# A hybrid decoder layer whose order a planner sets: other planning numbers, other pairs of outputs in PSUM banks, and two lists of tiles turned

## The chip, the cores and the metric

The kernel runs on one core of one Trainium2 chip. Its metric is the device time of one execution in microseconds, the median of several. A core has five engines that run their own instruction streams: TensorE (PE; its weight loads are shown as PEld), VectorE (DVE), ScalarE (ACT), GpSimd (POOL) and SyncE (SP), which here only issues DMAs. They meet in semaphores. Matmul results go to PSUM, eight banks of 512 fp32 numbers in each partition; everything else lies in SBUF.

## The reference

One decoder layer on 512 tokens of width 2048, in fp32. The conditioning vector `c` makes six modulation vectors through `w_ada`, 2048 x 12288 numbers, the largest matrix of the first stage.

```
mod_all = einsum('bd,ldm->lbm', silu(c), w_ada) + b_ada
h = rms_norm(x, norm1_g) * (1 + sc1) + sh1
u = h @ w_in                  # conv group, queries, keys and values of three branches, gates
y_conv = short_conv_mixer(u_b, u_c, u_h, conv_w, conv_b)
k_cmp = compress(rope(kc), cmp_pe_k, cmp_w1_k, cmp_w2_k)      # and v_cmp
y_attn = nsa_attention(q, k_cmp, v_cmp, k_slc, v_slc, k_win, v_win, gates)
x = x + g1 * ([rms_norm(y_conv) | rms_norm(y_attn)] @ w_out)
h = rms_norm(x, norm2_g) * (1 + sc2) + sh2
x = x + g2 * (square(relu(h @ w_ff1)) @ w_ff2)
return rms_norm(x, normf_g)
```

## The kernel before, in words

Every fp32 product is made of three matmuls in fp32r (`mm3`): high part times high part, high times low, low times high. So each weight tile of 128 x 1024 that a DMA brings is first split: ScalarE copies it to the high part, VectorE subtracts that from it for the low part (`weights`, `hilo`).

There are three stages, and each has a recorder of its own, an object of class `Order`, which stands in for the engines: a call is noted down with what it reads and writes, and all of it is put out at `emit`. In between, `plan` runs a list scheduler. It prices each instruction (`price`), gives each a due time (`late`), and always takes the instruction that can begin first. DMAs share one modelled wire, which moves `rate` bytes in a microsecond. The order in which the plan begins them is the order in which they stand on every engine; engines and queues then run in that order, whatever their real times are. Nearly all instructions are recorded, so they bear the line of the recorder's call, L123.

The first stage projects the normed tokens `h` with `w_kv`, `w_cv`, `w_conv`, `w_v` and `w_q` (tiles `raw`, split into `wh`; the compression weights are split into tiles called `sw`, in spare slots). Beside it run the 192 tiles of `w_ada`: SyncE loads one into a ring of tiles `wa`, and VectorE takes its product with `silu(c)` summed along the row (`dot`, a SCALAR_TENSOR_TENSOR `t,late<-wa,cs`, or `t,acc` for the first ones). From `part_done` on that ring has four tiles. A `wa` load carries a slack, `SLACK`: the plan begins it no sooner than so many microseconds after it is ready, its tile being free among other things. `more_ada` puts these loads in, along with the projections, at the places that the plan then moves.

The second stage is attention (scores `s` in three banks, values `pv`, transposes `pt`), with the output product of the convolution half (`pw`, two banks) filled in between. VectorE's first instructions there clear the tile `pc` of the first query block and read the first scores (`p<-s`).

The third stage starts with the output product of the attention half. Its first eight outputs (`pm`) take all eight banks `pf`, one each, for all 512 tokens. The second eight are made by `late_out`, for 256 tokens at a time: the first call for the low half, the second for the high half. An output of 256 tokens takes half a bank, 24 matmuls. The weights are kept in SBUF in between, in tiles called `hl`, `sg`, `gt` and `kw`. `residual` reads the result on VectorE and adds it to `x1`. Then come the two products of the feed-forward part, which are three fifths of the time. Their weight tiles pass through six staging tiles `rw`, taken in turn, as are the banks.

Of the kernel before, what the change touches and what calls it, by code (L numbers as in the profile page):

```python
# [16 lines left out]
P = 128  # L17
# [19 lines left out]
NSIDE = 7  # L37
NWA = 8
NBANK = 6
SLACK = 4.0  # L40
SOON = 10.0
BEHIND = 11.0

# [6 lines left out]
class Order:  # L50
# [2 lines left out]

    class Node:
        __slots__ = ("i", "eng", "call", "cost", "lag", "size", "preds", "succs", "late", "loose", "born",
                     "begin", "ready", "left", "lane", "slack", "due")

    def __init__(self, tc, tag, count, passes=1, pace=0.000456, rate=340e3):  # L60
        self.tc, self.tag, self.count, self.passes = tc, tag, count, passes
        self.lane, self.kept, self.slack, self.wide, self.pace = 0, set(), 0.0, (0.11, 0.00182), pace
        self.rate = rate
        self.nodes, self.past, self.seen, self.rings = [], {}, {}, {}
        self.outer, self.loose, self.due = set(), False, 0.0
        for e in ("tensor", "vector", "scalar", "sync", "gpsimd"):
            setattr(self, e, Order.Engine(self, e, getattr(tc.nc, e)))
# [132 lines left out]
    def plan(self, ideal, t, fixed):  # L200
        nodes = self.nodes
        ends = {}
        for name, by in self.seen.items():
            for i in set(by):
                ends.setdefault(i, []).append(name)
        users = {name: len(set(v)) for name, v in self.seen.items()}
        mine = sorted((n for x in nodes for n in x.born), key=lambda n: int(n.rsplit("_", 1)[1]))
        rank = {n: k for k, n in enumerate(mine)}

        for x in reversed(nodes):  # L210
            move = x.cost + x.lag if not x.size else 2.5 + x.size / self.rate
            x.late = min([nodes[s].late - (move if nodes[s].eng != "tensor" or x.eng != "tensor" else x.cost)
                          for s in x.succs] + [ideal.get(x.i, t + 10.0 - x.due)])

        free = dict.fromkeys(("tensor", "vector", "scalar", "sync", "gpsimd"), 0.0)
        wire = 0.0
        ready = {e: [] for e in free}
        lanes = {}
        for i in fixed or [x.i for x in nodes if x.eng == "tensor" and not x.loose]:
            lanes.setdefault(0 if fixed else nodes[i].lane, []).append(i)  # L220
        for lane in lanes.values():
            lane.reverse()
        slots = sorted([0.0] * (self.count - len(self.outer)))
        given = []
        while slots and len(given) < len(mine):
            given.append(slots.pop(0))
        for x in nodes:
            x.left, x.ready = len(x.preds), 0.0
            if not x.left and (x.eng != "tensor" or x.loose):
                ready[x.eng].append(x)  # L230
        out = []
        while len(out) < len(nodes):
            best = None
            for e in free:
                c = [(x, 0, None) for x in ready[e]]
                if e == "tensor":
                    c = [(x, -1, None) for x in ready[e]]
                    c += [(nodes[q[-1]], k, q) for k, q in lanes.items() if q and not nodes[q[-1]].left]
                for x, k, q in c:
                    at = max(free[e], x.ready + x.slack, wire - 2.0 if x.size else 0.0)  # L240
                    if x.born:
                        last = max(rank[n] for n in x.born)
                        if last >= len(given):
                            continue
                        at = max(at, given[last])
                    key = (at, k, x.late, x.i)
                    if best is None or key < best[0]:
                        best = key, x, q
            (at, *_), x, q = best
            e = x.eng  # L250
            if q is not None:
                q.pop()
            else:
                ready[e].remove(x)
            x.begin = at
            free[e] = at + x.cost
            end = at + x.cost + x.lag
            if x.size:
                wire = max(wire, at + 1.5) + x.size / self.rate
                end = wire + 0.7  # L260
            for n in ends.get(x.i, ()):
                users[n] -= 1
                if not users[n] and (n in rank or n in self.outer) and n not in self.kept:
                    if len(given) < len(mine):
                        given.append(max([end] + given[-1:]))
            for s in x.succs:
                y = nodes[s]
                y.left -= 1
                y.ready = max(y.ready, free[e] if e == y.eng == "tensor" else end)
                if not y.left and (y.eng != "tensor" or y.loose):  # L270
                    ready[y.eng].append(y)
            out.append(x)
        return max(free.values()), out
# [3 lines left out]
def hybrid_layer(ctx: ExitStack, tc: tile.TileContext, a, out):  # L277
# [38 lines left out]
        tc.keep_in_program_order(filler(nc.tensor))  # L316

    xs = [pair(name="x2") for _ in range(NK // 2)]
    nc = order = Order(tc, xs[0].tensor.tag, NMAIN, passes=6, pace=0.000444, rate=410e3)
    order.wide = (0.24, 0.0021)  # L320
    ts = [small.tile([P, T], F32, name="t", tag="t", bufs=5) for _ in range(5)]
    scr, temps = ts[0].bitcast(BF16), cycle(ts[1:])
# [797 lines left out]
    ffp = ffn.enter_context(tc.tile_pool(name="ffp", bufs=2, reuse_waits="tile"))  # L1120
    psf = ffn.enter_context(tc.tile_pool(name="psf", bufs=8, space=PSUM, reuse_waits="tile"))
    HT = T // 2
    rw = cycle([ffp.tile([P, 1024], F32, name="rw", bufs=6) for _ in range(6)])
    hl = cycle([ffp.tile([P, 2048 + 4 * SHIFT], F32R, name="hl", bufs=3) for _ in range(3)])

    class Low:
# [16 lines left out]
    gt = cycle([ffp.tile([P, 2, 2, HT], F32R, name="gt", bufs=3) for _ in range(3)])  # L1143
    gb = cycle([ffp.tile([P, 2, HT], F32R, name="gb", bufs=1)])
    p1s = cycle([ffp.tile([P, HT], F32, name="p1", bufs=3) for _ in range(3)])
    banks = cycle([psf.tile([P, T], F32, name="pf") for _ in range(8)])
    LO, HI = slice(0, HT), slice(HT, T)
    halves = (LO, HI)
    whole = slice(0, T)
# [1 line left out]
    def bankf():  # L1151
        return next(banks)
# [30 lines left out]
    def residual(ps, m, c):  # L1183
        xm = x1[m // 2][:, m % 2, c]
        nc.vector.scalar_tensor_tensor(out=xm, in0=ps, scalar=col(M_G1, m), in1=xm,
                                       op0=OP.mult, op1=OP.add)
        square_into(sacc, xm, c, m == 0)
# [27 lines left out]
            dst = [slot(F32R, name="kw")[:, :1024] for _ in range(2)]  # L1215
        kept.append(hilo(dst, raw_blob(a["w_oa2"][i])))
    def late_out(hf):
        ps = []
        for i in range(8):
            if i % 2 == 0:  # L1220
                ps.append(bankf())
            wh, wl = kept[i]
            for k in range(8):
                s = slice(k * P, (k + 1) * P)
                mm3(ps[-1][:, halves[i % 2]], wh[:, s], wl[:, s], mixa[k][:, 0, halves[hf]],
                    mixa[k][:, 1, halves[hf]], k == 0, k == 7)
        for i in range(8):
            c = halves[hf]
            residual(ps[i // 2][:, halves[i % 2]], 8 + i, c)
            if i % 2:  # L1230
                j = 4 + i // 2
                nc.gpsimd.dma_start(out=x1d[j][:, :, c], in_=x1[j][:, :, c])
# [416 lines left out]
```

## Time and profile before

| | |
|---|---|
| median of 3 executions | 2099.62 us (2099.16 to 2104.02) |
| profiled execution | 2096.75 us |
| its span, first to last instruction | 2095.0 us |
| mean granted TensorE clock | 0.991 |
| ScalarE, GpSimd busy | 1007.7 us (48%), 128.1 us (6%) |
| first stage | to about 557 us |
| attention with half the output product | to about 748 us |
| rest of the output product | to about 845 us |
| feed-forward part | to the end |

The span is what the profile shows of one execution; the execution's own time is 1.75 us longer. Rows of the timeline give start and length in microseconds, engine, line, operation, output and inputs by the program's names, shape, and in brackets how long the engine idled before and what ended that. Rows of waits give the waiting engine, its tile and line, what it waited for, and the total, the number and the longest. "Granted clock" is the share of TensorE's full clock that it was given.

### The profile page before, as it was taken

What the parts mean: (1) busy time and instruction counts of PE and PEld (TensorE: products, weight loads), DVE (VectorE), ACT (ScalarE), POOL (GpSimd) and SP (SyncE); (2) the same over time, 40 slices, a digit from 0 to 9 for tenths busy, and PEclk for the clock granted to TensorE, in tenths of its full rate; (3) what the DMA queues carried; (4) which work ended last, traced back from release to release, by engine and by line L of the source; (5) the groups of instructions that cost most, each with busy time, mean ns of one, the idle gap of its engine ahead of it and who ended that gap; (6) DMA issues with size and microseconds to landing.
All of it is one profiled execution on the core that took longest, in us unless ns stands there. A gap on an engine that the chain in (4) does not pass through costs nothing.

```text
span 2095.0 us, 38213 instructions
## 1 busy us (share of the span) xinstructions
PE 2054.9 (98%) x15038; PEld 1920.0 (92%) x15038; DVE 1885.9 (90%) x3104; ACT 1007.7 (48%) x1465; POOL 128.1 (6%) x244
## 2 busy tenths in 40 slices
PE   9999999999999999999999999999999999999997
PEld 7888787898788779999999999999999999999997
DVE  7999997887898657999999999999999999999998
ACT  4432333232465435776666666666443333333355
POOL 0000000000000001022211121222000000000000
PEclk8999999999999999999999999999999999999999
DMA  8986488888511134476766666668975466476452
GB/s 343 348 325 231 174 294 324 311 292 307 200 63 69 62 134 152 136 227 207 211 210 205 208 214 198 213 206 285 347 274 211 163 248 227 138 254 239 144 181 99
DMA packets 144276, 454.19 MB, mean 217 GB/s; under 512 B 15840, under 2 KB 20320, under 8 KB 144096
## 3 DMA queue, kind: packets, MB, share of 16 engines
q1 hardware_dynamic: 108960, 386.72, 52.7%
q0 software_dynamic: 34048, 63.98, 10.1%
q8 instruction: 118, 1.93, 0.4%
q10 hardware_dynamic: 1088, 1.05, 0.1%
q14 instruction: 62, 0.51, 0.1%
HBM read 383.53 MB, written 68.16 MB: 216 GB/s over the span
## 4 chain that ended last, share of the span: by engine, by line
PE 90%; DVE 4%; DMA 3%; ACT 1%; issue 1%; SPq 0%; DVEq 0%; ACTq 0%
PE pf L123 63%; PE ps L123 19%; PE pw L123 4%; PE pv L123 2%; PE s L123 2%; DMA wa<-in_w_ada 1%; PE pt L123 1%; DMA raw<-in_cmp_w 1%; DVE wh L123 1%; DVE t L123 1%; DMA raw<-in_w_conv 0%; DMA x<-in_xt 0%; DVE x L123 0%; ACT wh L123 0%; DVE vz L123 0%
## 5 line engine op out<-in xcount | busy, mean ns | idle before, releaser
L123 PE MATMUL pf<-tk,hl 128*128 128x256 f32 x10704 | 1218.7, 276 | 0.5 <-ACT t L123 0.5
L123 PEld LDWEIGHTS pf<-tk,hl 128*128 128x128 f32 x10704 | 1217.1, 188 | 0.8 <-ACT t L123 0.7
L123 ACT ACTIVATE hl<-rw 128x1024 fp32r<-128x1024 f32 x269 | 285.7, 1063 | 338.3 <-PE pf L123 291.0
L123 DVE TENSOR_TENSOR hl<-rw,hl 128x1024 fp32r<-128x1024 f32 (+2 forms) x351 | 336.4, 968 | 32.4 <-ACT hl L123 31.9
L123 ACT ACTIVATE hl<-sg 128x1024 fp32r<-128x1024 f32 x180 | 191.1, 1062 | 217.3 <-PE pf L123 170.0
L123 DVE SCALAR_TENSOR_TENSOR t<-wa,cs 128x1024 bf16<-128x1024 f32 x190 | 231.7, 1220 | 30.7 <-DMA wa<-in_w_ada 29.0
L123 PE MATMUL ps<-h_m,wh 128*128 128x512 f32 x1080 | 252.3, 390 | 0.9 <-DVE h_m L123 0.9
L123 PEld LDWEIGHTS ps<-h_m,wh 128*128 128x128 f32 x1080 | 201.1, 188 | 42.4 <-DVE h_m L123 1.3
L123 ACT ACTIVATE wh<-raw 128x1024 fp32r<-128x1024 f32 (+1 forms) x106 | 112.7, 1064 | 257.3 <-PE ps L123 214.8
L123 DVE TENSOR_TENSOR hl<-sg,hl 128x1024 fp32r<-128x1024 f32 (+2 forms) x193 | 188.2, 986 | 27.1 <-ACT hl L123 26.9
L123 PE MATMUL ps<-h,wh 128*128 128x512 f32 x840 | 198.9, 395 | 2.9 <-ACT h L123 2.9
L123 PEld LDWEIGHTS ps<-h,wh 128*128 128x128 f32 x840 | 159.5, 191 | 36.7 <-ACT h L123 3.5
L123 DVE TENSOR_TENSOR wh<-raw,wh 128x1024 fp32r<-128x1024 f32 (+1 forms) x106 | 129.7, 1224 | 21.8 <-ACT wh L123 21.1
L123 DVE TENSOR_TENSOR sg<-sg,rw 128x1024 f32<-128x1024 f32 x120 | 145.8, 1215 | 0.0
L123 DVE SCALAR_TENSOR_TENSOR x<-pf,mod,x 128x256 f32<-128x256 f32 (+1 forms) x280 | 130.0, 483 | 13.5 <-PE pf L123 11.6
L123 POOL DMA_DIRECT2D g<-gt x192 | 101.1, 532 | 424.3 <-ACT hl L123 185.7
L123 PE MATMUL pw<-mix,wh 128*128 128x512 f32 x384 | 110.7, 407 | 0.0
L123 ACT ACTIVATE t<-t 128x512 f32<-128x512 f32 (+3 forms) x131 | 74.8, 571 | 15.9 <-DVE t L123 13.8
L123 DVE TENSOR_TENSOR sg<-rw 128x1024 f32<-128x1024 f32 x60 | 73.1, 1219 | 7.9 <-DMA rw<-in_w_f 4.8
L123 PEld LDWEIGHTS pw<-mix,wh 128*128 128x128 f32 x384 | 69.2, 190 | 10.8 <-issue 0.5
L123 DVE TENSOR_TENSOR rw<-rw 128x1024 f32<-128x1024 f32 x60 | 72.9, 1215 | 0.0
L123 ACT ACTIVATE gt<-t 128x512 fp32r<-128x512 f32 x96 | 60.3, 629 | 18.1 <-DVE t L123 15.2
(217 smaller groups left out, 1775.6 us busy)
## 6 DMA issues: line engine op xcount, KB each, us to landing
rw<-in_w_f SPq DMA_DIRECT2D x263, 512.0 KB, 4.2
wa<-in_w_ada SPq DMA_DIRECT2D x192, 512.0 KB, 6.0
tk<-g SPq DMA_DIRECT2D x114, 512.0 KB, 6.6
g<-gt POOLq DMA_DIRECT2D x192, 256.0 KB, 5.3
raw<-in_w_conv SPq DMA_DIRECT2D x32, 512.0 KB, 4.0
x<-in_xt SPq DMA_DIRECT2D x16, 512.0 KB, 5.7
raw<-in_w_kv SPq DMA_DIRECT2D x16, 512.0 KB, 5.5
raw<-in_w_cv SPq DMA_DIRECT2D x16, 512.0 KB, 5.1
```

The costliest lines, as they stand in the source:

```text
L123: x.i, x.eng, x.call = len(self.nodes), eng, (lambda: real(*args, **kw))
```

## The change

Five edits. `SLACK` goes from 4 to 1. The planner's wire gets two rates in place of one for each stage: 340 thousand bytes a microsecond, and 410 while the modelled wire time is below `rush`; the first stage, which had 410 throughout, now has it for its first 40 modelled microseconds, and its due times always use 340. The other stages had 340 and keep it. In `late_out`, outputs i and i+4 share a bank, where 2j and 2j+1 did. The list of banks begins at its third name, and the list of `rw` tiles runs backwards behind its first.

```
-SLACK = 4.0
+SLACK = 1.0
...
+    RATE, RUSH = 340e3, 410e3
...
-    def __init__(self, tc, tag, count, passes=1, pace=0.000456, rate=340e3):
+    def __init__(self, tc, tag, count, passes=1, pace=0.000456, rush=0.0):
...
-        self.rate = rate
+        self.rush = rush
...
-            move = x.cost + x.lag if not x.size else 2.5 + x.size / self.rate
+            move = x.cost + x.lag if not x.size else 2.5 + x.size / Order.RATE
...
-                wire = max(wire, at + 1.5) + x.size / self.rate
+                wire = max(wire, at + 1.5)
+                wire += x.size / (Order.RUSH if wire < self.rush else Order.RATE)
...
-    nc = order = Order(tc, xs[0].tensor.tag, NMAIN, passes=6, pace=0.000444, rate=410e3)
+    nc = order = Order(tc, xs[0].tensor.tag, NMAIN, passes=6, pace=0.000444, rush=40.0)
...
-    rw = cycle([ffp.tile([P, 1024], F32, name="rw", bufs=6) for _ in range(6)])
+    rw = [ffp.tile([P, 1024], F32, name="rw", bufs=6) for _ in range(6)]
+    rw = cycle(rw[:1] + rw[:0:-1])
...
-    banks = cycle([psf.tile([P, T], F32, name="pf") for _ in range(8)])
+    banks = [psf.tile([P, T], F32, name="pf") for _ in range(8)]
+    banks = cycle(banks[2:] + banks[:2])
...
     def late_out(hf):
-        ps = []
+        ps = [bankf() for _ in range(4)]
         for i in range(8):
-            if i % 2 == 0:
-                ps.append(bankf())
             wh, wl = kept[i]
             for k in range(8):
                 s = slice(k * P, (k + 1) * P)
-                mm3(ps[-1][:, halves[i % 2]], wh[:, s], wl[:, s], mixa[k][:, 0, halves[hf]],
+                mm3(ps[i % 4][:, halves[i // 4]], wh[:, s], wl[:, s], mixa[k][:, 0, halves[hf]],
                     mixa[k][:, 1, halves[hf]], k == 0, k == 7)
         for i in range(8):
             c = halves[hf]
-            residual(ps[i // 2][:, halves[i % 2]], 8 + i, c)
+            residual(ps[i % 4][:, halves[i // 4]], 8 + i, c)
```

The planning numbers move instructions all through the first stage from about its tenth weight tile on; the second stage stands as it was, and the third differs only around `late_out`. Three places follow, each before and then after.

VectorE at the end of the first stage; its last row here is the first of attention. `mix` are the splits of the convolution half, `t,late<-wa,cs` are dots, `wh<-raw` is the low part of a weight tile:

```order
L123 TENSOR_TENSOR mix<-y,mix 128x512 x5
L123 TENSOR_TENSOR wh<-raw,wh 128x1024
L123 TENSOR_TENSOR mix<-y,mix 128x512 x3
L123 SCALAR_TENSOR_TENSOR t,late<-wa,cs 128x1024 x2
L123 TENSOR_TENSOR wh<-raw,wh 128x1024
L123 SCALAR_TENSOR_TENSOR t,late<-wa,cs 128x1024 x5
L123 TENSOR_TENSOR mod<-late 128x16
L123 TENSOR_TENSOR mod<-mod,vec 128x16
L123 MEMSET pc 128x96 x2
```

```order
L125 TENSOR_TENSOR mix<-y,mix 128x512 x6
L125 TENSOR_TENSOR wh<-raw,wh 128x1024
L125 SCALAR_TENSOR_TENSOR t,late<-wa,cs 128x1024 x3
L125 TENSOR_TENSOR wh<-raw,wh 128x1024
L125 SCALAR_TENSOR_TENSOR t,late<-wa,cs 128x1024
L125 TENSOR_TENSOR mod<-late 128x16
L125 TENSOR_TENSOR mod<-mod,vec 128x16
L125 TENSOR_TENSOR wh<-raw,wh 128x1024
L125 MEMSET pc 128x96 x2
```

The last two `wh<-raw` in each are those for the last `w_q` tile and the first tile of the convolution half's output weights, `w_oc`. Seven dots stood between the former and attention, and one stands there now; the three `mix` splits have moved ahead of it.

SyncE at the same place, the last loads ahead of the second stage's first load of `x`:

```order
L123 DMA wa<-in_w_ada 128x1024 x2
L123 DMA raw<-in_w_q 128x1024
L123 DMA wa<-in_w_ada 128x1024 x2
L123 DMA raw<-in_w_q 128x1024
L123 DMA wa<-in_w_ada 128x1024 x2
L123 DMA raw<-in_w_oc 128x1024
L123 DMA wa<-in_w_ada 128x1024 x4
L123 DMA raw<-in_w_oc 128x1024 x2
```

```order
L125 DMA wa<-in_w_ada 128x1024 x2
L125 DMA raw<-in_w_q 128x1024
L125 DMA wa<-in_w_ada 128x1024 x3
L125 DMA raw<-in_w_q 128x1024
L125 DMA wa<-in_w_ada 128x1024
L125 DMA raw<-in_w_q 128x1024 x2
L125 DMA raw<-in_w_oc 128x1024 x3
```

Six `wa` loads stood behind the last `w_q` load, four of them behind the first `w_oc` load; now none does, and between weight loads two or three stand where two did.

TensorE in the first call of `late_out`, from its third output (brackets name the engine whose semaphore a matmul waits for). The weights of the outputs are `hl`, then `sg`, `gt`, and `kw` for three:

```order
L123 MATMUL pf<-mixa,hl 128x256 x21
L123 MATMUL pf<-mixa,sg 128x256 x8
L123 MATMUL pf<-mixa,sg 128x256 [waits DVE_49]
L123 MATMUL pf<-mixa,sg 128x256 x15
L123 MATMUL pf<-mixa,gt 128x256 x24
L123 MATMUL pf<-mixa,kw 128x256 x2
L123 MATMUL pf<-mixa,kw 128x256 [waits DVE_49]
L123 MATMUL pf<-mixa,kw 128x256 x45
```

```order
L125 MATMUL pf<-mixa,hl 128x256 x21
L125 MATMUL pf<-mixa,sg 128x256 x24
L125 MATMUL pf<-mixa,gt 128x256 [waits DVE_49]
L125 MATMUL pf<-mixa,gt 128x256 x23
L125 MATMUL pf<-mixa,kw 128x256 [waits DVE_49]
L125 MATMUL pf<-mixa,kw 128x256 x23
L125 MATMUL pf<-mixa,kw 128x256 [waits DVE_49]
L125 MATMUL pf<-mixa,kw 128x256 x23
```

The waits for VectorE stood inside an output, behind its eighth or second matmul, for the read of the output just before it. Now they stand at an output's first matmul, for the read of the output four earlier.

## The prediction

> **What bounds the kernel now.** I read the page's first lines, then the windows of 50 us, then TensorE's own waits.
>
> ```profile
> span 2095.0 us, 38213 instructions
> ...
> PE 2054.9 (98%) x15038; PEld 1920.0 (92%) x15038; DVE 1885.9 (90%) x3104; ACT 1007.7 (48%) x1465; POOL 128.1 (6%) x244
> ...
> 200.00:250.00 50.00, 48.35 (x230) 39.74 (x229) 48.40 (x67) 20.89 (x25) 0.00 (x0) 1.00 0.39 135
> 250.00:300.00 50.00, 47.59 (x239) 39.19 (x238) 43.02 (x61) 18.86 (x23) 0.00 (x0) 1.00 0.83 303
> 300.00:350.00 50.00, 48.80 (x237) 39.86 (x236) 40.43 (x61) 16.11 (x17) 0.00 (x0) 1.00 0.86 311
> 350.00:400.00 50.00, 48.04 (x237) 39.45 (x236) 41.27 (x63) 14.27 (x19) 0.00 (x0) 1.00 0.86 318
> 400.00:450.00 50.00, 47.95 (x315) 43.77 (x314) 43.01 (x67) 15.06 (x22) 0.00 (x0) 1.00 0.82 290
> 450.00:500.00 50.00, 50.00 (x295) 44.78 (x294) 39.22 (x70) 11.18 (x17) 0.00 (x0) 1.00 0.89 315
> 500.00:550.00 50.00, 50.00 (x223) 41.40 (x222) 44.04 (x64) 18.09 (x25) 0.00 (x0) 1.00 0.73 253
> 550.00:600.00 50.00, 44.83 (x226) 38.24 (x225) 43.28 (x146) 24.91 (x71) 0.00 (x0) 0.90 0.33 116
> ...
> 850.00:900.00 50.00, 49.53 (x432) 49.28 (x431) 46.02 (x96) 37.19 (x69) 1.10 (x2) 1.00 0.39 127
> ```
>
> In the windows, the columns are the stretch, its length, the busy time of TensorE, of its weight loads, VectorE, ScalarE and GpSimd, the granted clock, the DMA share and GB/s. TensorE is busy for 2054.9 of 2095.0 us, so 40.1 us is all that a better order can win, and whatever delays TensorE is paid in full. Behind 850 us its windows are full to within half a microsecond; what is won ahead of that point should be kept. The idle time that this change can touch lies in two stretches: 200 to 450 us has 1.65 + 2.41 + 1.20 + 1.96 + 2.05 = 9.3 us, and 550 to 600 us has 5.2 us, in one piece, with the clock down to 0.90. TensorE's waits name the culprits (columns: total, times, longest):
>
> ```profile
> PE ps L123 <- ACT sw L123: 6.3, 7, 1.6
> PE s L123 <- DVE pc L123: 5.2, 1, 5.2
> PE pf L123 <- DVE x L123: 3.6, 5, 1.3
> ```
>
> The first are the compression weights `sw` in the first stage, the second is the door from the first stage to attention, the third mostly the second half of the output product.
>
> **The change part by part.**
>
> *Names that turn.* The reversed `rw` list and the rotated `banks` list change which name comes first. In the two built programs the tiles stand at the same places in the order of use: the first bank used is bank 0, then 7, 6, 5 and so on in both, and all 277 loads into `rw` go to the same addresses in the same order. So no wait moves and both cost 0. That the first matmul of the output product waits for the same VectorE update in both programs fits.
>
> *The door to attention.* The timeline there:
>
> ```profile
> 537.70 19.20 PE L123 MATMUL ps<-h,wh 128*128 128x512 f32 x84
> 547.90 1.22 DVE L123 TENSOR_TENSOR wh<-raw,wh 128x1024 fp32r<-128x1024 f32 x1
> 551.27 1.06 ACT L123 ACTIVATE wh<-raw 128x1024 fp32r<-128x1024 f32 x1 [3.81 <-PE ps L123]
> 554.90 2.64 ACT L123 ACTIVATE qr<-ps 128x512 f32<-128x512 f32 x4 [2.57 <-PE ps L123]
> 556.74 1.13 PE L123 MATMUL s<-kslc,q 128*128 128x160 f32 x9
> 557.71 0.91 PE L123 MATMUL pw<-mix,wh 128*128 128x512 f32 x3
> 561.01 1.22 DVE L123 SCALAR_TENSOR_TENSOR t<-wa,cs 128x1024 bf16<-128x1024 f32 x1 [1.59 <-DMA wa<-in_w_ada]
> 562.16 0.08 DVE L123 DVE_READ_ACCUMULATOR t<-wa,cs 128x1 f32 x1
> 562.63 0.25 DVE L123 MEMSET pc<- 128x96 f32 x2
> 563.35 0.28 DVE L123 CUSTOM_DVE_ANT_0 p<-s,causal 128x128 f32<-128x128 f32 x1
> 563.79 0.93 PE L123 MATMUL s<-kslc,q 128*128 128x160 f32 x3 [5.17 <-DVE pc L123]
> ```
>
> TensorE starts attention at 556.74, fills the three score buffers, does three `pw` matmuls, and then needs a score buffer back. VectorE reads the first one only at 563.35, since seven dots of the adaLN weights (1.22 + 0.08 us each), the last of which waits 1.59 us for its load, stand ahead of it. That is the 5.17 us.
>
> In the changed program all 192 `wa` loads are issued ahead of the last two `w_q` loads, where six followed before. Behind the subtraction for the last `w_q` tile stand one dot, two short sums and the subtraction for the first `w_oc` tile, in place of three `mix` splits, seven dots, those sums and that subtraction. With the subtraction at 547.90 as now, the first `w_oc` one can start when ScalarE has made its high part, 551.27 + 1.06 = 552.3, and VectorE is at the `pc` memset by 552.3 + 1.2 = 553.5, three microseconds ahead of the first scores. If it slips, the last `w_q` tile is needed 24 x 19.20/84 = 5.5 us before 556.7, at 551.2, so it has some 2 us. What is late next is the score buffer itself: the first one is full by about 557.2, its read takes 0.28, and the three `pw` matmuls cover until 558.5. So the whole **5.2 us** goes. Its cover is VectorE's room earlier: it must do six dots and three splits, 6 x 1.30 + 3 x 0.62 = 9.7 us, ahead of the last `w_q` subtraction that it now does behind it; between 450 and 550 us it idles for 10.8 + 6.0 = 16.8 us. If that room isn't usable, the stall only moves (first rival).
>
> With the stop goes the clock that it costs:
>
> ```profile
> 558.00:560.00 2.00, 0.61 (x3) 0.17 (x1) 1.39 (x4) 0.00 (x0) 0.00 (x0) 1.00 1.01 354
> 560.00:562.00 2.00, 0.00 (x0) 0.00 (x0) 0.99 (x1) 0.00 (x0) 0.00 (x0) 0.61 0.99 387
> 562.00:564.00 2.00, 0.21 (x1) 0.22 (x2) 1.93 (x11) 0.34 (x2) 0.00 (x0) 0.50 1.03 420
> 564.00:570.00 6.00, 6.00 (x23) 5.52 (x24) 3.53 (x25) 4.13 (x17) 0.00 (x0) 0.50 0.28 113
> 570.00:575.00 5.00, 5.00 (x28) 4.44 (x28) 3.93 (x18) 1.89 (x6) 0.00 (x0) 0.93 0.18 36
> ```
>
> From 564 to 570 TensorE has work all the time at clock 0.50, and to 575 at 0.93: 6 x 0.5 + 5 x 0.07 = **3.3 us** lost if these matmuls were bound by TensorE alone, nothing if the softmax chain would have held them anyway. I take 3.3, since TensorE shows no idle time there. [...]
>
> *The output product's second half.* Before, outputs 2j and 2j+1 lie in the halves of one bank. VectorE reads the first half for the residual while TensorE writes the second, and the two are kept apart by whole bank:
>
> ```profile
> 805.35 0.48 DVE L123 SCALAR_TENSOR_TENSOR x<-pf,mod,x 128x256 f32<-128x256 f32 x1 [0.49 <-PE pf L123]
> 805.89 2.15 PE L123 MATMUL pf<-mixa,sg 128*128 128x256 f32 x16 [0.58 <-DVE x L123]
> 811.67 6.02 PE L123 MATMUL pf<-mixa,kw 128*128 128x256 f32 x48 [0.57 <-DVE x L123]
> 818.27 2.89 PE L123 MATMUL pf<-mixa,kw 128*128 128x256 f32 x22 [0.58 <-DVE x L123]
> 843.48 1.82 PE L123 MATMUL pf<-mixa,kw 128*128 128x256 f32 x13 [0.58 <-DVE x L123]
> ```
>
> Four stops of 0.58 us. With outputs i and i+4 in a bank, the residual has three outputs' time to read. In the first call each wait's VectorE row stands some 80 instructions ahead of it and is long done. In the second call one stop in mid-output stays: the fourth set of matmuls of output 4 waits for the residual of output 0, placed just ahead. Three of four go: 3 x 0.58 = **1.7 us**.
>
> *The plan of the first stage.* The planner prices its loads at 340 GB/s behind the first 40 us instead of 410, and holds `wa` loads 1 us instead of 4 behind a free tile. Which is nearer the chip? The windows from 250 to 400 us move 303 to 318 GB/s at shares of 0.83 to 0.86, some 365 per full share: 410 is too fast by 12%, 340 too slow by 7%. So `sw` tiles were promised too early, and TensorE stood for them seven times; now they are promised too late, and TensorE is given other matmuls until then. Against that stands the smaller reserve:
>
> ```profile
> SPq L123 <- DVE wh L123: 130.6, 35, 6.7
> ...
> SPq L123 <- DVE t L123: 14.8, 9, 5.3
> ```
>
> These are SyncE's own waits between 200 and 450 us. SyncE issues in order; a `wa` load whose tile isn't free (the second row) holds the weight loads behind it. Runs of three `wa` loads between weight loads become usual where two were. Neither row prices the new order, so I bound it: all 9.3 us of idle from 200 to 450 us gone at one end, as much again added at the other. I take **2 us** won, a third of the 6.3 us of `sw` waits; the better rate speaks for more, the thinner reserve for less.
>
> **The sum.** 5.2 + 3.3 + 1.7 + 2.0 = 12.2 us. The profiled execution took 2096.75 us (span 2095.0), so its successor takes 2084.5. The median shown, 2099.62, stands 2.9 us higher; on that footing the forecast is **2087 us**.
>
> **The rivals.**
>
> *The stall moves.* The dots are pulled ahead, but VectorE's idle time in the first stage is time in which their loads have not landed:
>
> ```profile
> L123 DVE SCALAR_TENSOR_TENSOR t<-wa,cs 128x1024 bf16<-128x1024 f32 x189 | 230.5, 1220 | 29.2 <-DMA wa<-in_w_ada 27.4
> ```
>
> Of the dots' idle time in the first 560 us, 27.4 us is waiting for `wa`. Then the subtractions for the last `w_q` tiles come late and TensorE stops there for what it no longer stops at the door. For it: the 16.8 us of room are partly such waits. Against it: the loads go out earlier, and from 500 to 550 us the DMA share is only 0.73. The 5.2 and 3.3 us stay, 1.7 + 2.0 are won: 2096.
>
> *SyncE is held (slower).* Every `wa` load issued too early holds a weight load. It decides if each of the 16 `sw` tiles costs TensorE the longest wait now seen, 1.6 us: 25.6 in place of 6.3, so 19.3 lost, 5.2 + 3.3 + 1.7 won, 2109. Below about 10 us lost there, the result is not slower than now. For it: the 5.3 us hold above. Against it: most holds are by `wh`, which the reserve doesn't touch.
>
> *Nothing in sum.* The new plan loses in the first stage what the door and the output product win, about 10 us: 2100. The two turned lists do nothing in any case.
>
> **How the numbers follow.** The forecast has 0.64, the moved stall 0.14, no sum 0.12, the held queue 0.10. About 0.3% (6.3 us) is what a measurement of this kernel can tell from no change, so faster ends at 2093.3 and slower begins at 2105.9. The forecast's own range is 2080 (all 9.3 us of the first stage won, 7.3 more than taken) to 2093; the moved stall and most of the third case reach to 2100. The range is 2080 to 2100. Faster: 0.64 and a little of the moved stall, 0.66; slower 0.10; same 0.24.
>
> **What would show it.** Right: from 556 to 575 us TensorE has no gap above 1 us and the granted clock stays at 1.00; no dot stands between the first scores and the first score read; in the output product one stop for `x` in the second call and none in the first; the stretch from 850 us on as long as before. Wrong: waits of TensorE for `wh` or `sw` in the first stage that sum to more than now, SyncE's waits for `t` well above 14.8 us between 200 and 450 us, or a gap at the door that VectorE doesn't explain.

## The result, and the profile after

The changed kernel takes 2080.94 us (median of 6 runs, 2078.09 to 2083.80), the kernel before in the same set 2099.29 us (6 runs, 2096.21 to 2104.02): a ratio of 0.9911, with a 95% interval from 0.9897 to 0.9925, so 18.4 us less. The profiled execution took 2083.80 us, the longest of the six, with a span of 2082.0 us. Between the two profiled executions the difference is 13.0 us, and the gain of the medians is 5.4 us larger; where that comes from is taken up below.

The page's first lines, and TensorE's own waits over the whole run (columns as before: total, times, longest). The helper line that was L123 is L125 now.

```profile
span 2082.0 us, 38227 instructions
...
PE 2053.3 (99%) x15038; PEld 1919.7 (92%) x15038; DVE 1885.2 (91%) x3104; ACT 1007.8 (48%) x1465; POOL 128.4 (6%) x244
```

```profile
PE ps L125 <- ACT sw L125: 2.6, 3, 2.0
PE pf L125 <- DVE x L125: 1.9, 2, 1.3
PE ps L125 <- DVE sw L125: 1.8, 2, 1.6
```

TensorE's idle time is 2082.0 - 2053.3 = 28.7 us, where it was 40.1. The wait of `s` for VectorE's `pc` is gone from the list, the waits for `sw` are 2.6 + 1.8 = 4.4 us where they were 7.0, and those for `x` have halved.

The windows of 50 us, in the columns of before (TensorE's busy time is the first number behind the comma, the granted clock stands third from the end):

```profile
200.00:250.00 50.00, 48.44 (x231) 40.08 (x230) 49.21 (x67) 21.02 (x25) 0.00 (x0) 1.00 0.49 163
250.00:300.00 50.00, 49.31 (x248) 40.79 (x247) 45.01 (x66) 19.94 (x24) 0.00 (x0) 1.00 0.88 308
300.00:350.00 50.00, 49.40 (x251) 40.97 (x250) 43.88 (x63) 15.92 (x17) 0.00 (x0) 1.00 0.92 328
350.00:400.00 50.00, 47.97 (x221) 39.36 (x220) 40.25 (x64) 14.43 (x19) 0.00 (x0) 0.97 0.89 313
400.00:450.00 50.00, 49.30 (x340) 45.86 (x339) 45.03 (x70) 15.10 (x22) 0.00 (x0) 1.00 0.91 321
...
500.00:550.00 50.00, 50.00 (x223) 41.38 (x222) 43.46 (x65) 18.16 (x26) 0.00 (x0) 1.00 0.59 216
550.00:600.00 50.00, 50.00 (x272) 42.17 (x271) 45.83 (x156) 32.39 (x90) 0.00 (x0) 1.00 0.21 74
...
850.00:900.00 50.00, 49.05 (x427) 48.66 (x426) 47.87 (x97) 36.81 (x63) 5.34 (x10) 1.00 0.57 177
```

Idle from 200 to 450 us is 1.56 + 0.69 + 0.60 + 2.03 + 0.70 = 5.6 us, down from 9.3, and the DMA share in that stretch is higher. The window from 550 to 600 us is full, at clock 1.00. The timeline shows the door:

```profile
547.40 1.23 DVE L125 TENSOR_TENSOR wh<-raw,wh 128x1024 fp32r<-128x1024 f32 x1 [2.65 <-ACT wh L125]
548.60 0.24 DVE L125 MEMSET pc<- 128x96 f32 x2
...
551.78 1.13 PE L125 MATMUL s<-kslc,q 128*128 128x160 f32 x9
552.27 0.29 DVE L125 CUSTOM_DVE_ANT_0 p<-s,causal 128x128 f32<-128x128 f32 x1 [1.02 <-PE s L125]
...
553.48 0.46 PE L125 MATMUL s<-kslc,q 128*128 128x160 f32 x3
```

VectorE sets `pc` 3.2 us ahead of the first scores, no dot stands behind that, and it now waits for the scores. From the first scores to the fourth score it is 553.48 - 551.78 = 1.7 us, where it was 563.79 - 556.74 = 7.05: 5.35 us less. In the second half of the output product the first call has no stop for `x`, and the second has one:

```profile
820.48 1.92 PE L125 MATMUL pf<-mixa,gt 128*128 128x256 f32 x14 [0.58 <-DVE x L125]
```

The part behind it is about as long as before: from the first matmul of the feed-forward part to the end it is 2095.0 - 845.13 = 1249.9 us before, 2082.0 - 830.87 = 1251.1 us after, and 1249.7 us in a second profile of the changed kernel (e9_again).

One sign named in advance as speaking against the change did appear. These are SyncE's waits between 200 and 450 us:

```profile
SPq L125 <- DVE wh L125: 95.2, 33, 6.7
SPq L125 <- DVE t L125: 56.8, 47, 4.5
```

Its waits for dots (`t`) rose from 14.8 to 56.8 us, but those for `wh` fell by 35.4, and TensorE waits less than before.

### The profile page after: what moved, and what is told of

It reads as the page before. It is cut to its first block, busy times and chain, and to the rows that moved or that the text cites. A ratio compares the mean times of both kernels' runs of the same rounds, so it can differ in the third digit from the quotient of the medians.

```text
span 2082.0 us, 38227 instructions
## 1 busy us (share of the span) xinstructions
PE 2053.3 (99%) x15038; PEld 1919.7 (92%) x15038; DVE 1885.2 (91%) x3104; ACT 1007.8 (48%) x1465; POOL 128.4 (6%) x244
## 4 chain that ended last, share of the span: by engine, by line
PE 91%; DMA 4%; DVE 3%; ACT 1%; issue 1%; SPq 0%; DVEq 0%; ACTq 0%
PE pf L125 62%; PE ps L125 20%; PE pw L125 4%; PE pv L125 2%; PE s L125 2%; PE pt L125 1%; DMA wa<-in_w_ada 1%; DMA raw<-in_cmp_w 1%; DMA tk<-g 1%; DVE wh L125 1%; DMA rw<-in_w_f 0%; DVE t L125 0%; DMA x<-in_xt 0%; ACT wh L125 0%; DVE ct L125 0%
## 5 line engine op out<-in xcount | busy, mean ns | idle before, releaser
L125 PE MATMUL pf<-tk,hl 128*128 128x256 f32 x10704 | 1219.1, 276 | 1.3 <-DVE hl L125 0.8
L125 PEld LDWEIGHTS pf<-tk,hl 128*128 128x128 f32 x10704 | 1217.3, 188 | 1.8 <-DVE hl L125 1.0
L125 ACT ACTIVATE hl<-rw 128x1024 fp32r<-128x1024 f32 x269 | 285.7, 1063 | 342.8 <-PE pf L125 297.6
L125 DVE TENSOR_TENSOR hl<-rw,hl 128x1024 fp32r<-128x1024 f32 (+2 forms) x351 | 336.0, 967 | 33.4 <-ACT hl L125 32.9
L125 ACT ACTIVATE hl<-sg 128x1024 fp32r<-128x1024 f32 x180 | 191.2, 1063 | 220.6 <-PE pf L125 159.0
L125 PE MATMUL ps<-h_m,wh 128*128 128x512 f32 x1080 | 252.4, 390 | 0.0
L125 DVE SCALAR_TENSOR_TENSOR t<-wa,cs 128x1024 bf16<-128x1024 f32 x190 | 231.5, 1219 | 18.1 <-DMA wa<-in_w_ada 16.3
L125 PEld LDWEIGHTS ps<-h_m,wh 128*128 128x128 f32 x1080 | 201.2, 188 | 41.8 <-DVE h_m L125 0.4
L125 ACT ACTIVATE wh<-raw 128x1024 fp32r<-128x1024 f32 (+1 forms) x106 | 112.8, 1065 | 260.6 <-PE ps L125 216.2
L125 DVE TENSOR_TENSOR hl<-sg,hl 128x1024 fp32r<-128x1024 f32 (+2 forms) x193 | 188.1, 985 | 26.8 <-ACT hl L125 26.6
L125 PE MATMUL ps<-h,wh 128*128 128x512 f32 x840 | 199.4, 395 | 2.9 <-ACT h L125 2.9
L125 PEld LDWEIGHTS ps<-h,wh 128*128 128x128 f32 x840 | 159.4, 191 | 36.7 <-ACT h L125 3.5
L125 DVE TENSOR_TENSOR wh<-raw,wh 128x1024 fp32r<-128x1024 f32 (+1 forms) x106 | 129.7, 1225 | 22.4 <-ACT wh L125 21.5
L125 DVE TENSOR_TENSOR sg<-sg,rw 128x1024 f32<-128x1024 f32 x120 | 145.7, 1214 | 0.0
L125 DVE SCALAR_TENSOR_TENSOR x<-pf,mod,x 128x256 f32<-128x256 f32 (+1 forms) x280 | 129.4, 483 | 11.5 <-PE pf L125 9.8
L125 POOL DMA_DIRECT2D g<-gt x192 | 101.4, 533 | 422.8 <-issue 188.3
L125 PE MATMUL pw<-mix,wh 128*128 128x512 f32 x384 | 109.5, 404 | 0.0
L125 ACT ACTIVATE t<-t 128x512 f32<-128x512 f32 (+3 forms) x131 | 74.7, 571 | 15.2 <-DVE t L125 13.1
L125 DVE TENSOR_TENSOR sg<-rw 128x1024 f32<-128x1024 f32 x60 | 73.0, 1217 | 7.1 <-DMA rw<-in_w_f 5.0
L125 PEld LDWEIGHTS pw<-mix,wh 128*128 128x128 f32 x384 | 68.6, 189 | 10.8 <-issue 0.5
L125 DVE TENSOR_TENSOR rw<-rw 128x1024 f32<-128x1024 f32 x60 | 72.8, 1214 | 0.0
L125 ACT ACTIVATE gt<-t 128x512 fp32r<-128x512 f32 x96 | 60.2, 628 | 13.9 <-DVE t L125 11.2
```

Of the source, the lines that this page charges most:

```text
L125: x.i, x.eng, x.call = len(self.nodes), eng, (lambda: real(*args, **kw))
```

## The experiments

All ratios are against the kernel before in the same set, with 95% intervals; a median is that of 4 to 12 executions.

| run | us, median | ratio |
|---|---|---|
| e1_slack | 2085.11 | 0.9929 (0.9917 to 0.9942) |
| e2_rate | 2099.20 | 0.9992 (0.9982 to 1.0003) |
| e3_late | 2096.59 | 0.9987 (0.9976 to 0.9997) |
| e4_names | 2099.09 | 0.9997 (0.9987 to 1.0006) |
| e5_fill | 2096.26 | 0.9988 (0.9976 to 1.0000) |
| e6_busy | 2091.28 | 0.9959 (0.9947 to 0.9972) |
| e7_slack2 | 2080.64 | 0.9907 (0.9894 to 0.9920) |
| e8_rate365 | 2089.61 | 0.9950 (0.9938 to 0.9963) |
| e9_again | 2081.02 | 0.9904 (0.9888 to 0.9920) |
| e10_slack3 | 2089.69 | 0.9940 (0.9921 to 0.9959) |
| e11_first365 | 2082.94 | 0.9909 (0.9891 to 0.9928) |
| e12_plan | 2082.42 | 0.9909 (0.9893 to 0.9925) |

From each profile, by the same three starts in the timelines (first score, fourth score, first matmul of the output product) and TensorE's idle time ahead of the fourth score, in us:

| profile | first score at | idle at the door | fourth score to output product |
|---|---|---|---|
| before | 556.7 | 5.17 | 184.8 |
| e3_late | 557.2 | 6.72 | 183.4 |
| e4_names | 556.8 | 3.76 | 186.3 |
| e5_fill | 557.0 | 0.83 | 181.6 |
| e2_rate | 549.3 | 11.18 | 185.7 |
| e1_slack | 551.8 | 0 | 181.7 |
| after | 551.8 | 0 | 181.5 |
| e9_again | 550.4 | 0 | 181.6 |
| e12_plan | 547.5 | 0 | 181.4 |
| e6_busy | 548.8 | 7.58 | 183.4 |
| e7_slack2 | 549.2 | 0 | 181.5 |
| e10_slack3 | 551.2 | 1.39 | 181.7 |
| e8_rate365 | 551.3 | 0 | 185.6 |
| e11_first365 | 552.7 | 0 | 181.7 |

### One part at a time

**e1_slack**

```
-SLACK = 4.0
+SLACK = 1.0
```

> The kernel before with SLACK = 1.0 alone; the loads are still priced at 410 GB/s. In its program no dot stands between the subtraction for the last w_q tile and the pc memset (seven before). Theory A (the thinner reserve is what empties the door): no gap of TensorE at the first scores and clock 1.00 behind it, 8.5 us won there; the first stage is not helped by the rate, so 0 to 4 us are lost there to SyncE held by wa tiles: 2087 to 2092. Rival (the stall moves to the last w_q tiles): within 3 us of the kernel before, with a new wait of TensorE for wh between 450 and 550 us.

About 15 us of the 18.4 come with this one number, so the time lies below the 2087 to 2092 expected. The door is open. But the first stage did not lose the 0 to 4 us expected: it became 4.9 us shorter, as in the profile after. SyncE's `wa` loads show what happened. The three fences are the kernel before, this run and the changed kernel; the last two times are the starts of the first and the last of the 192 loads:

```profile
L123 SPq DMA_DIRECT2D wa<-in_w_ada x192: 327/384/1530, 5.6 to 555.7; - x192
```

```profile
L123 SPq DMA_DIRECT2D wa<-in_w_ada x192: 327/328/553, 6.3 to 493.3; - x192
```

```profile
L125 SPq DMA_DIRECT2D wa<-in_w_ada x192: 327/328/1483, 6.2 to 518.6; - x192
```

The last `wa` load goes out at 555.7 us before, at 493.3 with the smaller reserve alone, and at 518.6 with both numbers changed. Before, SyncE's timeline near the end of the stage reads:

```profile
515.95 1.95 SPq L123 DMA_DIRECT2D wa<-in_w_ada  x3
...
538.51 0.33 SPq L123 DMA_DIRECT2D raw<-in_w_oc  x1
541.46 14.52 SPq L123 DMA_DIRECT2D wa<-in_w_ada  x4
```

Four `wa` loads are left behind the first `w_oc` load, and issuing them takes 14.52 us, since each waits for a dot to free its tile (between 538 and 558 us SyncE waits for `t` four times, 15.5 us in total). The dots stand on VectorE behind the splits and subtractions of the last weights, and from 517 to 559 us VectorE never idles for more than 0.2 us. Earlier in the stage it had time to spare, which its dots spent waiting for `wa` loads. In total and in number, over the whole run, these waits are, for the kernel before, this run and the changed kernel:

```profile
  DVE t L123: 29.0, 26
```

```profile
  DVE t L123: 6.4, 10
```

```profile
  DVE t L125: 16.3, 17
```

With the smaller reserve the loads come sooner, the dots are done in that time, and fewer are left for the end.

A `wa` load now often stands ahead of a weight load that would be held for `wh` anyway, so part of SyncE's hold only changes its name. In this run, between 200 and 450 us:

```profile
SPq L123 <- DVE t L123: 99.7, 88, 3.2
SPq L123 <- DVE wh L123: 74.7, 37, 6.6
```

`t` and `wh` together are 174.4 us here, 152.0 in the changed kernel and 130.6 + 14.8 = 145.4 before. SyncE is held for longer, and TensorE's waits for `sw` nevertheless fell, from 7.0 us to 3.6 here and 4.4 in the changed kernel.

**e2_rate**

```
-                wire = max(wire, at + 1.5) + x.size / self.rate
+                wire = max(wire, at + 1.5)
+                wire += x.size / (Order.RUSH if wire < self.rush else Order.RATE)
```

with RATE 340e3, RUSH 410e3 and `rush=40.0` for the first stage, SLACK still 4.0.

> The kernel before with the two rates (410 GB/s for the first 40 us, 340 behind) and SLACK still 4.0. Its program has seven dots in a row ahead of the pc memset, as before. Theory A: the gap of 5 us at the first scores stays and so does the low clock behind it; only TensorE's waits for sw in the first stage shrink, by 2 to 5 us: 2094 to 2098. Rival (the rate is what pays, the reserve nothing): 2090 or less, or the gap gone.

The time is that of the kernel before within the interval, above the 2094 to 2098 expected, and yet TensorE reaches the first scores at 549.3 us, 7.4 us sooner. All of it is lost in one wait:

```profile
PE s L124 <- DVE pc L124: 11.2, 1, 11.2
```

The fourth score is set at 563.8 us in both profiles. The last `wa` load goes out at 555.7 us in both, so the dots end at the same time, and whatever TensorE gains ahead of the door it spends waiting there. The row says more than was expected of it: with this order of loads the door opens when VectorE is through with its dots, the last of which hang on the last `wa` loads, and what TensorE waits in the first stage costs nothing in the end. Part of the 7.4 us may be bought there: eleven `wa` loads stand behind the first `w_oc` load in this program, where four stood in the kernel before. Whether TensorE's waits cost that kernel anything, with its own order of loads, is not shown.

**e3_late**

```
-        ps = []
+        ps = [bankf() for _ in range(4)]
...
-                mm3(ps[-1][:, halves[i % 2]], wh[:, s], wl[:, s], mixa[k][:, 0, halves[hf]],
+                mm3(ps[i % 4][:, halves[i // 4]], wh[:, s], wl[:, s], mixa[k][:, 0, halves[hf]],
```

and the same indices in the residual.

> The kernel before with outputs i and i+4 in one bank in the second half of the output product, and nothing else. Theory A: three of the four stops of 0.58 us go, 1.7 us won, 2097.6; the one left is in the second call. Rival (VectorE is late next, and TensorE stops for it elsewhere): no difference.

The ratio gives 2.7 us, with an interval from 0.6 to 5.0 us that holds the 1.7. Its waits for `x` between 735 and 860 us are two, the longer at the start of the output product, so one of the four stops is left:

```profile
PE pf L123 <- DVE x L123: 1.9, 2, 1.3
```

e12_plan, below, measures the same part a second time.

**e4_names**

```
+    rw = cycle(rw[:1] + rw[:0:-1])
...
+    banks = cycle(banks[2:] + banks[:2])
```

> The kernel before with the turned rw list and the rotated banks list alone. Theory: the same places in the same order of use, so the same time, within 1.5 us of the kernel before, and this shows how far two equal programs come out apart. Rival (the places do differ, and a bank is waited for elsewhere): a difference of 2 us or more in either direction, with other waits at the start of the output product.

No difference. Its profile is of use in another way. The order of VectorE's work is that of the kernel before, and still the wait at the door is 3.8 us in place of 5.2:

```profile
PE s L123 <- DVE pc L123: 3.8, 1, 3.8
```

while the clock stays low for longer behind it:

```profile
565.00:570.00 5.00, 5.00 (x22) 4.79 (x22) 2.35 (x15) 2.71 (x9) 0.00 (x0) 0.50 0.02 7
570.00:575.00 5.00, 5.00 (x22) 4.37 (x21) 4.96 (x23) 1.88 (x6) 0.00 (x0) 0.73 0.32 105
```

### The door by itself

**e5_fill**

```
+            if i == self.hook:
+                self.fill()
...
+    def fill():
+        for _ in range(5):
+            tc.keep_in_program_order(tc.nc.tensor.matmul(spare, ones, ones[:, None, :].to_broadcast([P, NQ, P]),
+                                                         start=True, stop=True))
```

The hook is the first matmul of the fourth score.

> The kernel before; ahead of the fourth score of attention, where TensorE stands idle for 4 to 7 us, it does five extra matmuls of ones into the bank of pv, which is not in use yet (0.85 us each at full clock, 4.3 us in all, which nothing reads). VectorE's order is unchanged. Theory A (the low clock behind the gap is lost time on its own): the gap shrinks to 1 or 2 us, the fourth score is no later, the granted clock stays near 1.00 behind it, and from the fourth score to the output product it is about 3 us shorter: about 2096. Rival (behind the gap TensorE would have been held by the softmax chain in any case): clock 1.00, but the same length from the fourth score on, and new waits of TensorE for VectorE or ScalarE between 564 and 600 us: 2099.

In its timeline and its windows:

```profile
558.74 4.45 PE L981 MATMUL pv<-ones 128*128 128x512 f32 x10
564.02 0.56 PE L124 MATMUL s<-kslc,q 128*128 128x160 f32 x3 [0.83 <-DVE pc L124]
```

```profile
564.00:570.00 6.00, 5.98 (x41) 5.60 (x42) 5.54 (x31) 5.36 (x21) 0.00 (x0) 1.00 0.38 152
570.00:575.00 5.00, 5.00 (x29) 4.26 (x28) 4.60 (x26) 2.50 (x9) 0.00 (x0) 1.00 0.29 105
```

The five extra matmuls take 4.45 us, where 4.3 were expected. The fourth score is no sooner (564.0, first score 557.0), but the clock is 1.00, TensorE does 41 matmuls from 564 to 570 us where it did 23, and from the fourth score to the output product it takes 181.6 us, as long as with an open door, not 184.8. So the 3.2 us are the clock's and not the softmax chain's. The time agrees (0.9988, 2.5 us with an interval from 0 to 5.0).

**e6_busy**

```
     order.emit()
+    for _ in range(16):
+        tc.keep_in_program_order(tc.nc.vector.tensor_tensor(out=ts[0], in0=causal, in1=causal, op=OP.max))
     proj.close()
```

> The changed kernel with 16 VectorE operations on scratch (0.6 us each, some 9.6 us, which nothing reads) between the first stage and the pc memset, so that VectorE comes to the first score as late as in the kernel before; loads, plan and output product are those of the changed kernel. Theory A (the door cost 8.5 us, gap and clock): the gap is back with about 5.5 us, the clock is near 0.50 behind it, and the time is 8 to 9 us above the changed kernel: 2089 to 2090. Rival (attention has slack behind the door and takes the gap in): at most 3 us above it.

```profile
549.78 0.91 PE L125 MATMUL pw<-mix,wh 128*128 128x512 f32 x3
558.27 0.93 PE L125 MATMUL s<-kslc,q 128*128 128x160 f32 x3 [7.58 <-DVE pc L125]
```

The gap is 7.58 us, 2 us larger than expected, because the first scores came at 548.8 us and not at 551.8; the time, 2091.28, lies above the expected 2089 to 2090 for the same reason. The granted clock is 0.53 from 555 to 560 us. From the first score to the output product it is 192.8 us against 183.2 in the profile after, 9.6 us more; the two ratios differ by 0.0048, 10.1 us. Attention has no slack that would take in a late start.

### The plan's numbers

**e7_slack2** and **e10_slack3**: the changed kernel with `SLACK = 2.0` and with `SLACK = 3.0`.

> The changed kernel with SLACK = 2.0 in place of 1.0. In its program six dots stand behind the subtraction for the last w_q tile but two, and none between the last two subtractions for w_q and w_oc and the memset. With SLACK 4.0 and these rates the first scores came at 549.3 us, with 1.0 at 551.8. Theory (the reserve costs TensorE a little in the first stage, and only the end of the wa stream matters at the door): first scores between those, at about 550.5, door open, 2079 to 2081. Rival (the last wa loads are late again): a gap at the door of 2 us or more, 2083 to 2090.

> The changed kernel with SLACK = 3.0. In its program seven dots stand behind the last w_q subtraction but one and ahead of the memset, four and three about the last one. The last wa load was issued at 518.6 us with 1.0, at 539.0 with 2.0 and at 555.7 with 4.0. Theory (the end of the wa stream decides, and by nothing until it reaches the first scores): the last wa load at 545 to 553 us, first scores at 549; a gap of 0 to 4 us at the door, 2081 to 2089. Rival (the reserve costs by itself, all along the first stage): the first scores move to 552 or later, halfway to the kernel before.

With 2.0 the last `wa` load goes out at 539.0 us, the door stays open, and the time equals the changed kernel's. With 3.0 it goes out at 546.4, the fourth score waits 1.39 us, and the time is 0.9940, outside the expected 2081 to 2089 by a little. That fits an end of the `wa` stream that costs nothing until it reaches the door. But the size doesn't fit: its median stands 8.7 us above e9_again's and its profiled span 7.4 us, of which 1.6 us are at the door and 0.8 at the first score; 4.6 us are scattered in the feed-forward part, where its order is that of the changed kernel. Where those come from stays open; from its first matmul to the end that part takes 1254.3 us in this profile and 1249.7 to 1252.8 us in the thirteen others.

**e8_rate365** and **e11_first365**: the changed kernel with `RATE` 365e3 in all plans, and in the first stage alone.

> The changed kernel with its loads priced at 365 GB/s behind the first 40 us in place of 340 (what the windows of the kernel before moved per full share). Its program has no dot in the last 20 rows ahead of the memset. Theory (the price of a load matters little once the wa stream ends early): first scores at 550 to 553 us, door open, within 2 us of the changed kernel. Rival (340 is what keeps the sw tiles in time): waits for sw back to 6 us, first scores at 555 or later, 2084 or more.

> The changed kernel with 365 GB/s behind the first 40 us in the first stage alone; the later plans have their 340 back, whose loss at the start of the output product (a stop of 5.3 us, since fewer pw matmuls were kept as cover) made the run with 365 everywhere useless as a test of the first stage. Theory (the price matters little in the first stage): attention and the output product as in the changed kernel, first scores at 549 to 552 us, 2080 to 2084. Rival (340 keeps the sw tiles in time): waits for sw of 4 us or more, 2084 to 2087.

The first of them missed, for a reason that has nothing to do with the first stage: its first scores came at 551.3 us with the door open. RATE belongs to all the plans, and at the start of the output product this one left 28 `pw` matmuls in the last run of them, where the changed kernel has 46:

```profile
726.40 6.95 PE L125 MATMUL pw<-mix,wh 128*128 128x512 f32 x28
738.65 1.19 PE L125 MATMUL pf<-mixa,wh 128*128 128x512 f32 x2 [5.30 <-DVE x L125]
```

From the fourth score to the output product this costs 4.1 us. By the ratios the time is 8.2 us above the changed kernel's, and where the rest comes from stays open.

With 365 in the first stage alone the time is within 2 us of e9_again's, and the waits for `sw` are 3.6 us. So the door doesn't hang on 340 against 365. The first stage may, by a little: the first scores came at 552.7 us, outside the expected 549 to 552 and later than in the four profiles of the changed kernel's order below, which lie 4.3 us apart among themselves.

**e9_again** is the changed kernel itself, and **e12_plan** leaves out of it the new pairing and the two turned lists.

> The changed kernel itself, for a second profile and beside the three others of this set. Theory (its first profile had one stop of 2.0 us at 355 us and low clock behind it that most of its executions lack): first scores at 549 us, as in the program with 16 operations more behind the same first stage (548.8), and 2079 to 2082 us. Rival (551.8 us is where its first stage ends, and the gain left over lies elsewhere): first scores at 551.5 or later again.

> The changed kernel without the new pairing in the output product and without the two turned lists: SLACK 1.0 and the two rates alone, the same order of matmuls in the first stage. Theory (terms add): 1.7 us above the changed kernel of this set, with four stops of 0.58 us for x back in the output product, 2082 to 2084. Rival (the pairing gives the 2.7 us that its own run showed, or nothing once the rest has moved): 2085 or more, or the time of the changed kernel.

e9_again has its first scores at 550.4 us, between the two expected values. The median of e12_plan is 1.4 us above e9_again's, a difference that lies within the intervals of the two; the stops for `x` are back in e12_plan, between 735 and 860 us:

```profile
PE pf L124 <- DVE x L124: 2.3, 4, 0.6
```

Four programs now share one order of the first stage (after, e6, e9, e12): 551.8, 548.8, 550.4 and 547.5, on average 549.6 us to the first score. Four share the old one (before, e3, e4, e5): 556.7, 557.2, 556.8 and 557.0, on average 556.9. The first stage gained 7.3 us, and the profile after shows 4.9 of it, since its execution was the slowest of the four there.

## Why the prediction came out as it did

Its direction, its likeliest case and its range held: 2080.94 lies in 2080 to 2100, at the edge. The forecast of 2087 was 6 us too high, and one term of the sum accounts for most of that.

**The turned lists** were put at 0, and e4_names measures 0.6 us of difference with an interval that spans zero. Right.

**The door**, 5.2 + 3.3 = 8.5 us. Measured, from the first score to the output product: 191.8 us before (7.0 + 184.8), 183.2 after, 8.6 us. The two parts stand separately as well: e5_fill gives back the clock's part alone and e6_busy closes the door again. Right in mechanism and in size. The size of the clock's part by itself was luck: behind the gap, against the 181.5 us of an open door, the lost time was 3.3 us in the kernel before, 1.9 in e3, 4.8 in e4, 4.2 in e2 and 1.9 in e6, and the row that was used lies near their mean of 3.2. The sum of gap and clock is steadier: the kernel before, e3 and e4 share one order, wait 5.2, 6.7 and 3.8 us, and need 191.8, 192.0 and 191.9 us from the first score to the output product. Why the shorter wait had the longer low clock, the runs don't show.

**The output product**, 1.7 us. Measured as 2.7 (e3) and 1.4 (e12 against e9), neither of them sharply, with one stop left where it was foretold. The profiles tell more, from the first matmul of the output product to the first of the feed-forward part. The clock falls at the start of this stretch in some profiles, as the last section shows, so like is compared with like. Without that, it is 96.4 to 96.9 us with the old pairing (before, e2, e5) and 94.1 and 94.4 with the new (e11, e7); with it, 97.9 to 98.4 (e1, e4, e12) and 95.7 to 96.0 (after, e3, e6, e9, e10). The means differ by 2.4 and by 2.3 us. Right in mechanism, and 0.6 us short; what a stop costs beyond its 0.58 us was not traced.

**The plan of the first stage**, put at 2.0 us out of bounds of 9.3 either way: this is the step that was mis-sized; the first scores came 7.3 us sooner. The prediction said that "the better rate speaks for more, the thinner reserve for less". The first half holds: the rate alone brought the first score 7.4 us forward (e2). The second half doesn't: with the old rate the thinner reserve alone brought it 4.9 us forward (e1), and with the new one no loss can be seen (549.3 us with 4.0, 551.2 with 3.0, 549.2 with 2.0, 549.6 on average with 1.0; single profiles of one order lie up to 4.3 us apart). The term was also cut from too small a piece, a third of the waits for `sw`. These fell by 2.6 us between the two profiles, while TensorE's idle time in all windows up to 550 us fell by 4.8 us.

A second fault didn't show in the number. The prediction added this term to the door's as if the two were independent. e2_rate shows that they need not be: with the door shut by the dots, 7.4 us won ahead of it came to 0.0008 of the time. The two could be added here only because the same edit moved the end of the `wa` stream from 555.7 to 518.6 us. For the changed program the prediction did work out when VectorE would set `pc`, 553.5 us, but held that against first scores at 556.7; against scores at 549.6 us it would have been a shut door again. The door stayed open because `pc` was set at 548.6 us (after), 547.2 (e9) and 544.3 (e12).

**The stall moves**, the first rival, did not come: from 450 to 550 us TensorE is busy without a gap in the profile after, and none of its listed waits in the first stage is for `wh`.

**SyncE held**, the slower rival, had its sign and not its effect: the waits for `t` rose fourfold. The sign was badly chosen; the waits of TensorE for what SyncE loads were the ones to watch.

One reading of the prediction was too wide: behind 850 us TensorE's windows in the kernel before are full only up to 2050 us, and in the last 45 us it is busy for 32.5. The change doesn't touch that end, so nothing of the sum hung on it.

With the measured terms the sum is 8.6 + 7.3 + 2.3 = 18.2 us, against 18.4 measured by the medians; with terms from a few profiles each, so close a match is partly luck. The two profiles show 13.0: 5.0 us up to the first score, 8.6 from there to the output product and 0.7 in it, less 1.3 us in the feed-forward part. The profiled execution before lay 2.5 us under its median and the one after 2.9 us over; 2.2 us of the latter are in its first stage (551.8 against 549.6).

**No run beats the changed kernel** by what can be measured; e7_slack2 is level with it.

## What to carry to other kernels

A wait at the border between two stages is better read as a time (when it ends) than as a length: ask what its releaser hangs on, and whether anything won ahead of the border moves that too. If not, the win is swallowed whole, as the 7.4 us of e2_rate were. A low-priority stream that must end by a certain point should be pulled into holds that its queue has anyway, since here TensorE did not wait more for it (for `sw` 4.4 us, where it was 7.0), though SyncE's holds grew (for `t` and `wh` between 200 and 450 us, from 145.4 to 152.0 us). And a stop of some microseconds is best counted with the clock behind it (at the door 1.9 to 4.8 us more, behind stops of 3.8 to 11.2 us), which can be tested by itself with idle matmuls in the gap.

## What the runs showed of the hardware

Stops much shorter than the one at the door (5.17 us in the kernel before) lowered the clock too, and in some executions only. At the start of the output product TensorE stops for 1.30 and 1.00 us, 0.70 us apart. In the profile after, the timeline has the stops, and windows of one microsecond show the clock:

```profile
734.98 0.70 PE L125 MATMUL pf<-mixa,wh 128*128 128x512 f32 x2 [1.30 <-DVE x L125]
736.68 12.14 PE L125 MATMUL pf<-mixa,wh 128*128 128x512 f32 x46 [1.00 <-DVE wh L125]
```

```profile
736.00:737.00 1.00, 0.32 (x1) 0.32 (x2) 1.00 (x2) 0.00 (x0) 0.00 (x0) 0.69 0.00 0
737.00:738.00 1.00, 1.00 (x3) 0.81 (x3) 0.76 (x1) 0.00 (x0) 0.00 (x0) 0.50 0.00 0
738.00:739.00 1.00, 1.00 (x4) 0.71 (x4) 0.00 (x0) 0.00 (x0) 0.00 (x0) 0.50 0.00 0
739.00:740.00 1.00, 1.00 (x4) 0.82 (x3) 0.00 (x0) 0.00 (x0) 0.00 (x0) 0.61 0.00 0
740.00:741.00 1.00, 1.00 (x6) 0.81 (x6) 0.00 (x0) 0.00 (x0) 0.00 (x0) 1.00 0.00 0
```

Of the granted clock 0.31 + 0.50 + 0.50 + 0.39 = 1.7 us are missing there, and the 46 matmuls behind the second stop take 12.14 us. In the kernel before the same place has as much idle time (stops of 1.27 and 0.99 us), and no loss:

```profile
746.00:748.00 2.00, 1.29 (x6) 0.75 (x4) 2.00 (x4) 0.85 (x1) 0.00 (x0) 1.00 0.00 0
748.00:750.00 2.00, 0.70 (x2) 0.30 (x2) 2.00 (x3) 0.21 (x1) 0.00 (x0) 1.00 0.00 0
750.00:752.00 2.00, 1.74 (x8) 1.43 (x9) 1.34 (x2) 0.00 (x0) 0.00 (x0) 1.00 0.00 0
```

Stops like these lower the clock there in 8 of 13 profiles (e8, whose first stop is longer, left out): the 46 matmuls take 12.1 to 12.4 us in those eight and 10.7 us in the five others. In e7 and e11 the same two stops, as long (2.26 and 2.30 us of idle time in all), do not lower it: the clock is 1.00 from 730 to 755 us. So such a loss costs about 1.5 us. That it sets the time of an execution is not shown: of the six executions of the changed kernel the slowest (2083.80 us) had the lowest mean clock, 0.992, but in e9_again the clock was 0.993 in five, and 0.994 in the second slowest.

So in the profile after 2.3 us of idle time within 3.0 us were enough to lower the clock, and in the kernel before, in e7 and in e11 as much of it was not; what decides it, the runs don't show.
